# A two-layer encoder trunk: the output projections with one 512-column product per step

## The chip, the core and the metric

The kernel runs on one core of one Trainium2 chip. The metric is device time in microseconds: the median of several executions. TensorE (PE in the profile, its weight loads PEld), VectorE (DVE), ScalarE (ACT), GpSimd (POOL) and SyncE (SP, which here issues the DMAs) each run their own queue of instructions in order and wait for one another by semaphores. TensorE multiplies a 128x128 weight tile, loaded first, with a moving operand of up to 512 columns and adds the result up in PSUM.

## The reference

Two layers over 256 tokens of width 2048. Each layer normalises its input, projects it into the inputs of two groups of heads, computes the groups, gates them, and sends the 2048 gated columns through one output projection whose result is added to the layer's input. A last norm follows.

```python
for l in range(DEPTH):
    h = rms_norm(x, norm_g[l])
    proj = jnp.einsum('btd,dc->btc', h, w_in[l])
    ...                       # RWKV-7 time mixing -> y_rw, windowed attention -> y_at
    mix = jnp.concatenate([y_rw * jax.nn.silu(g_rw), y_at * jax.nn.silu(g_at)], axis=-1)
    x = x + jnp.einsum('btc,cd->btd', mix, w_out[l])
return rms_norm(x, final_g)
```

The change is in the last product, `mix` times `w_out`.

## The kernel before

Everything is kept transposed: 128 channels on the partitions, the 256 tokens along the row. A matrix of width 2048 is thus 16 rows (`kk` or `k` = 0 to 15) of 128x256.

**Products in three parts.** To keep single precision, each operand is split into a high part (rounded to the float32r type that TensorE multiplies in one pass) and a low part (what the rounding left). A product of weight W and operand X is computed as Wh Xh + Wh Xl + Wl Xh: the three lines L309, L310 and L311 of `step` in `gemm`. One output tile of 128 channels is 16 such steps, 48 products, all added up in one PSUM tile `pm` (128x256, two buffers in turn). A weight tile comes in two halves of 8 steps. `wload` (L231) starts the DMA of a half from DRAM into one of three `raw` buffers, `wsplit` makes `hi` on ScalarE (L239) and `lo` on VectorE (L241), in two pieces of 512 columns each, into one of two buffers.

**The stream.** `Stream` holds the list of all weight halves of the whole kernel, input and output projections, and runs one step at a time. PE's order is the order in which the code is written. The scans of the time mixing and the attention are written as generators, and `window` runs pieces of them between steps of the stream. The other engines' instructions are ordered by priorities.

**The output projection.** The gated columns `mix` are 16 rows, split like all operands: the high parts in `MH`, the low parts in `ML`. Rows 0 to 7 (time mixing) are written at the end of `scan_b`, rows 8 to 15 (attention) by `mix_split` (L681 to L683). In the profile the first eight rows are MHa and MLa, the others MHb and MLb. `queue_output` puts 16 tiles (`k`) in the stream. By the counts of the stream, the attention ends just as the first output tile begins; while the output tiles run nothing else is on PE. After a tile's last product, `evac` adds the residual on VectorE (L641) to get the new row x. In layer 0 ScalarE and VectorE split x for the next layer (`x_split`, L203 and L204) and a DMA copies it to DRAM (L650); in both layers ScalarE squares it (L655) and VectorE adds up the squares for the norm (L657). `begin` loads the residual row of a tile from DRAM when the tile begins (L635).

The names in the rows of the profile: pm the PSUM tile, hi and lo the split weights, raw the loaded ones, vg (layer 0) or X2a and X2b (layer 1) the residual row and then the new x, XH and XL the split x of the input projections, mf the squares. L1125, L1112, L216 and L994, which the prediction uses for comparison, are products of the attention (values), its transposes, the sums of the norm and a product of the scan.

Of the kernel before, what the change touches and what calls it, by code (L numbers as in the profile page):

```python
# [21 lines left out]
T = 256  # L22
# [111 lines left out]
def hybrid_trunk_kernel(ctx, tc, xT, wi, wv, wo, par, fing, dup, iup, sink, pos, cst, out):  # L134
# [47 lines left out]
    class Rows:  # L182
# [11 lines left out]
        def __getitem__(self, at):  # L194
# [3 lines left out]
                return self.t[k.start // n][p, k.start % n : (k.stop - 1) % n + 1, t]  # L198
            return self.t[k // n][p, k % n, t]

    def x_split(XH, XL, x, k, l):
        g = G0[:, k : k + 1] if l == 0 else PR[:, l, P_NG + k : P_NG + k + 1]
        A.activation(XH[:, k, :], x, AF.Copy, scale=g)  # L203
        V.scalar_tensor_tensor(XL[:, k, :], x, g, XH[:, k, :].bitcast(F32), op0=ALU.mult, op1=ALU.subtract)  # L204
# [87 lines left out]

    S = Stream()

    def gemm(src, operands, evac, raws=None, begin=None, bank=None):

        box = []

        def step(kk):
            def f(w):  # L300
                if not box:
                    box.append(bank() if bank else ps_main.tile([128, T], F32, tag="m", name="pm"))
                    if begin:
                        begin()
                pm = box[0]
                rh, rl = operands()
                k = kk % 8
                wh, wl = w[0][:, k * 128 : (k + 1) * 128], w[1][:, k * 128 : (k + 1) * 128]
                PE.matmul(pm, wh, rh[:, kk, :], start=(kk == 0), stop=False)  # L309
                PE.matmul(pm, wh, rl[:, kk, :], start=False, stop=False)  # L310
                PE.matmul(pm, wl, rh[:, kk, :], start=False, stop=(kk == 15))  # L311
# [313 lines left out]
    def queue_output(l):  # L625

        L = layers[l]
        last = l + 1 == DEPTH

        def tile_of(k):  # L630
            xs = []

            def begin():
                xs.append(st("vg", [T], bufs=8))
                SY.dma_start(out=xs[0], in_=L.xin[:, k, :])  # L635

            def evac(pm):
                if last and k == 0:
                    L.X2 = Rows("s3", F32, "X2")
                x = L.X2[:, k, :] if last else xs[0]  # L640
                V.tensor_tensor(x, pm, xs[0], op=ALU.add)  # L641
                to = end if last else layers[l + 1]
                if k == 0:
                    to.norm = Norm()
                    to.acc = st("acc", [T])
                    if not last:
                        to.XH, to.XL = Rows("s2", F32R, "XH"), Rows("s3", F32R, "XL")
                if not last:
                    x_split(to.XH, to.XL, x, k, l + 1)
                    SY.dma_start(out=L.xd[:, k, :], in_=x)  # L650
                if k == 0:
                    A.activation(to.acc, x, AF.Square)
                else:
                    sq = st("mf", [T])
                    A.activation(sq, x, AF.Square)  # L655
                    if k < NKT - 1:
                        V.tensor_tensor(to.acc, to.acc, sq, op=ALU.add)  # L657
                    else:
                        to.sums = [to.acc, sq]
                if last:  # L660
                    A.activation(x, x, AF.Identity, scale=FG[:, k : k + 1])
                elif k == NKT - 1:
                    S.later(7, lambda: to.norm.add(to.sums))
                    S.later(14, lambda: to.norm.spread())

            return evac, begin

        for k in range(NKT):
            ev, be = tile_of(k)
            gemm(wo[l, k], lambda: (L.MH, L.ML), ev, begin=be)  # L670

    def layer(l):
        L = layers[l]
        prm = lambda o, j: PR[:, l, o + j : o + j + 1]
        dpm = lambda o, j: DP[:, l, o + j : o + j + 1]
        L.MH, L.ML = MH, ML = Rows("s1", F32R, "MH", 1), Rows("s0", F32R, "ML", 1)
# [294 lines left out]
        def scan_b(p, t):  # L971
# [77 lines left out]
            PA.activation(MH[:, p, :], Zt, AF.Copy)  # L1049
            yield  # L1050
            PV.tensor_tensor(ML[:, p, :], Zt, MH[:, p, :].bitcast(F32), op=ALU.subtract)
            yield

        chains = {}
# [73 lines left out]
        def attend():  # L1128

            scores(0)  # L1130
            yield
            flip(0)
            scores(1)
            yield
            for x in (MH, ML):
                x.more()
# [145 lines left out]
```

## Time and profile before

| | |
|---|---|
| time, median of 3 runs | 1171.67 us (1170.61 to 1172.37) |
| the profiled execution | 1171.01 us, its span 1169.2 us |
| PE busy in the span | 1148.4 us, 16151 products and as many weight loads |
| output projection of layer 0 | about 497 to 588 us of the span |
| output projection of layer 1 | about 1067 to 1157 us of the span |
| DVE, ACT busy | 905.4 us, 785.5 us |

A row of the timeline gives the start in us from the span's start, the duration, the engine, the line of the code, the operation, output<-inputs, the shape and, in brackets, how long the engine sat idle before and for whom. The ends of products are modelled and products overlap: their pace is read from their starts. A row of a tile gives the shortest, median and longest duration in ns and the first and last start in us. The granted clock is the share of TensorE's full clock that the throttle let through.

### The profile page before, as it was taken

What the parts mean: (1) busy time and instruction counts of PE and PEld (TensorE: products, weight loads), DVE (VectorE), ACT (ScalarE), POOL (GpSimd) and SP (SyncE); (2) the same over time, 40 slices, a digit from 0 to 9 for tenths busy, and PEclk for the clock granted to TensorE, in tenths of its full rate; (3) what the DMA queues carried; (4) which work ended last, traced back from release to release, by engine and by line L of the source; (5) the groups of instructions that cost most, each with busy time, mean ns of one, the idle gap of its engine ahead of it and who ended that gap; (6) DMA issues with size and microseconds to landing.
All of it is one profiled execution on the core that took longest, in us unless ns stands there. A gap on an engine that the chain in (4) does not pass through costs nothing.

```text
span 1169.2 us, 38101 instructions
## 1 busy us (share of the span) xinstructions
PE 1148.4 (98%) x16151; PEld 1074.6 (92%) x16151; DVE 905.4 (77%) x2012; ACT 785.5 (67%) x1986; POOL 21.7 (2%) x23
## 2 busy tenths in 40 slices
PE   8999999999999999999999999999999999999996
PEld 7988999999899999899999899999999999899996
DVE  7889978888877677766668888888887767786554
ACT  6667876787776666655556677876786666675553
POOL 0000000000000000000000000000000000000000
PEclk9999999999999999999999999999999999999998
DMA  7544334333333433477655443334333343346653
GB/s 261 168 152 134 130 106 127 97 112 113 96 116 124 134 120 121 141 238 234 212 177 176 141 135 116 106 108 131 98 112 111 121 136 122 106 144 191 213 192 127
DMA packets 60554, 166.63 MB, mean 143 GB/s; under 512 B 7744, under 2 KB 22880, under 8 KB 60384
## 3 DMA queue, kind: packets, MB, share of 16 engines
q1 hardware_dynamic: 60384, 164.21, 43.8%
q8 instruction: 126, 2.06, 0.7%
q14 instruction: 44, 0.36, 0.1%
HBM read 157.37 MB, written 4.19 MB: 138 GB/s over the span
## 4 chain that ended last, share of the span: by engine, by line
PE 75%; issue 13%; DVE 5%; ACT 4%; DMA 1%; SPq 0%; POOL 0%; POOLq 0%; DVEq 0%; ACTq 0%
PE pm L309 19%; PE pm L311 16%; PE pm L310 16%; PE pg L831 3%; PE pcc L994 2%; DVE lo L241 2%; PE pcc L1022 2%; PE pd L938 1%; PE py L1006 1%; PE py L979 1%; PE pq L929 1%; PE pcc L1012 1%; ACT hi L239 1%; DMA raw<-wi 1%; PE pza L689 1%
## 5 line engine op out<-in xcount | busy, mean ns | idle before, releaser
L241 DVE TENSOR_TENSOR lo<-raw,hi 128x512 fp32r<-128x512 f32 x560 | 372.0, 687 | 115.2 <-ACT hi L239 109.8
L239 ACT ACTIVATE hi<-raw 128x512 fp32r<-128x512 f32 x560 | 329.5, 625 | 169.7 <-PE pm L310 98.0
L309 PE MATMUL pm<-XHa,hi 128*128 128x256 f32 x832 | 245.6, 295 | 0.8 <-ACT VA L587 0.4
L309 PE MATMUL pm<-XHb,hi 128*128 128x256 f32 x832 | 243.5, 293 | 0.2
L311 PE MATMUL pm<-XHb,lo 128*128 128x256 f32 x832 | 234.2, 281 | 1.4 <-DVE lo L241 1.4
L311 PE MATMUL pm<-XHa,lo 128*128 128x256 f32 x832 | 234.1, 281 | 1.2 <-DVE lo L241 1.0
L310 PE MATMUL pm<-XLb,hi 128*128 128x256 f32 x832 | 234.0, 281 | 0.4 <-DVE XLb L204 0.4
L310 PE MATMUL pm<-XLa,hi 128*128 128x256 f32 x832 | 234.2, 281 | 0.1
L309 PEld LDWEIGHTS pm<-XHa,hi 128*128 128x128 f32 x832 | 157.1, 189 | 11.4 <-ACT XHa L203 1.3
L309 PEld LDWEIGHTS pm<-XHb,hi 128*128 128x128 f32 x832 | 157.0, 189 | 6.0 <-ACT hi L239 0.3
L311 PEld LDWEIGHTS pm<-XHa,lo 128*128 128x128 f32 x832 | 157.2, 189 | 2.5 <-DVE lo L241 2.4
L311 PEld LDWEIGHTS pm<-XHb,lo 128*128 128x128 f32 x832 | 157.2, 189 | 2.1 <-DVE lo L241 2.0
L310 PEld LDWEIGHTS pm<-XLa,hi 128*128 128x128 f32 x832 | 157.4, 189 | 0.7 <-DVE XLa L204 0.7
L310 PEld LDWEIGHTS pm<-XLb,hi 128*128 128x128 f32 x832 | 157.3, 189 | 0.6 <-DVE XLb L204 0.6
L1017 ACT ACTIVATE suv<-pcc 64x128 f32<-64x128 f32 x128 | 34.5, 270 | 72.3 <-PE pcc L1015 48.4
L309 PE MATMUL pm<-MHa,hi 128*128 128x256 f32 x256 | 72.0, 281 | 0.0
L311 PE MATMUL pm<-MHb,lo 128*128 128x256 f32 x256 | 71.8, 280 | 0.0
L310 PE MATMUL pm<-MLa,hi 128*128 128x256 f32 x256 | 71.8, 280 | 0.0
L310 PE MATMUL pm<-MLb,hi 128*128 128x256 f32 x256 | 71.7, 280 | 0.0
L309 PE MATMUL pm<-MHb,hi 128*128 128x256 f32 x256 | 71.7, 280 | 0.0
L311 PE MATMUL pm<-MHa,lo 128*128 128x256 f32 x256 | 71.7, 280 | 0.0
L309 PEld LDWEIGHTS pm<-MHa,hi 128*128 128x128 f32 x256 | 48.2, 188 | 0.8 <-issue 0.8
(291 smaller groups left out, 2322.7 us busy)
## 6 DMA issues: line engine op xcount, KB each, us to landing
raw<-wi SPq DMA_DIRECT2D x207, 512.0 KB
raw<-wo SPq DMA_DIRECT2D x64, 512.0 KB
raw<-wv SPq DMA_DIRECT2D x8, 512.0 KB
rrot<-u SPq DMA_DIRECT2D x80, 32.0 KB
vg<-xT SPq DMA_DIRECT2D x16, 128.0 KB
xd<-vg SPq DMA_DIRECT2D x16, 128.0 KB
vg<-xd SPq DMA_DIRECT2D x16, 128.0 KB
g<-dup SPq DMA_DIRECT2D x16, 97.0 KB
```

Of the source, the lines that this page charges most:

```text
L239: A.activation(hi[:, q], raw[:, q], AF.Copy)
L241: V.tensor_tensor(lo[:, q], raw[:, q], hi[:, q].bitcast(F32), op=ALU.subtract)
L309: PE.matmul(pm, wh, rh[:, kk, :], start=(kk == 0), stop=False)
L310: PE.matmul(pm, wh, rl[:, kk, :], start=False, stop=False)
L311: PE.matmul(pm, wl, rh[:, kk, :], start=False, stop=(kk == 15))
L689: PE.matmul(o, w[0], x[0], start=True, stop=False)
L831: PE.matmul(pg[:, h, c * 128 : (c + 1) * 128], BK[half[h], d, c, 1 - h : 3 - h, :].rearrange("p s j -> p (s j)"), MV[half[h], d, c].rearra ...
L929: PE.matmul(narrow(pq[:, d], h ^ d, c), hq(AB, d, c, h), sub(TC, h, d, c, d * b), start=True, stop=True)
L938: PE.matmul(narrow(pd[:, d], h, c), hx(TT, d, c, h), sub(QF, h ^ d, d, c, d * b), start=True, stop=True)
L994: PE.matmul(pc[half[h], 0, d, :], GE[h][r, d, ci[d], 0, :], SUV[r, d, ci[d], h, :], start=True, stop=True)
L1017: A.activation(here(h), pc[half[h], 1], AF.Copy)
L1022: PE.matmul(pS[half[h], d, :], BT[:, h, d, i, :], SUV[:, d, ci[d], h, :], start=(i == 0), stop=True, skip_group_check=True)
```

## The change

The split rows of `mix` no longer lie in two arrays, high and low, but side by side: row `kk` of `L.M` (class `Pairs`, four rows per tile, tiles M0 to M3) is 512 columns, 256 high and then 256 low. In 15 of 16 output tiles of each layer (`wide`) `pm` is 128x512, and a step has two products: the high weights with all 512 columns (Wh Xh into the first half, Wh Xl into the second), and the low weights with the 256 high columns, added to the first half. The evacuation then takes two additions on VectorE: residual plus first half, and that plus second half. The last tile of each layer keeps three products and one addition.

```diff
+    class Pairs:
+        def more(self):
+            for tag in (("s0a", "s1a"), ("s0b", "s1b"))[len(self.t) // 2]:
+                self.t.append(hold(tag, F32R, "M" + str(len(self.t)), (4, 2, T)))
+        def row(self, j, part=None):
+            t = self.t[j // 4][:, j % 4]
+            return t.rearrange("p a t -> p (a t)") if part is None else t[:, part]
...
-                    box.append(bank() if bank else ps_main.tile([128, T], F32, tag="m", name="pm"))
+                    box.append(bank() if bank else ps_main.tile([128, 2 * T if wide else T], F32, tag="m", name="pm"))
...
+                if wide:
+                    m = pairs()
+                    PE.matmul(pm, wh, m.row(kk), start=(kk == 0), stop=(kk == 15), skip_group_check=True)
+                    PE.matmul(pm[:, 0:T], wl, m.row(kk, 0), start=False, stop=(kk == 15), skip_group_check=True)
+                    return
...
-                V.tensor_tensor(x, pm, xs[0], op=ALU.add)
+                V.tensor_tensor(x, pm[:, 0:T], xs[0], op=ALU.add)
+                if k < NKT - 1:
+                    V.tensor_tensor(x, x, pm[:, T : 2 * T], op=ALU.add)
...
-            gemm(wo[l, k], lambda: (L.MH, L.ML), ev, begin=be)
+            gemm(wo[l, k], None, ev, begin=be, pairs=lambda: L.M, wide=k < NKT - 1)
...
-            A.activation(MH[:, j, :], mf, AF.Copy)
-            V.tensor_tensor(ML[:, j, :], mf, MH[:, j, :].bitcast(F32), op=ALU.subtract)
+            A.activation(L.M.row(j, 0), mf, AF.Copy)
+            V.tensor_tensor(L.M.row(j, 1), mf, L.M.row(j, 0).bitcast(F32), op=ALU.subtract)
```

On PE, the end of layer 0's first output tile (step 15) and the first step of the second stand so before:

```order
L309 MATMUL pm_9537<-MHb_8529,hi_9560 128x256 [waits Activation_49]
L310 MATMUL pm_9537<-MLb_8530,hi_9560 128x256 [waits DVE_49]
L311 MATMUL pm_9537<-MHb_8529,lo_9561 128x256
L309 MATMUL pm_9614<-MHa_331,hi_9592 128x256 [waits Activation_49]
L310 MATMUL pm_9614<-MLa_332,hi_9592 128x256
L311 MATMUL pm_9614<-MHa_331,lo_9593 128x256 [waits DVE_49]
```

and so in the changed kernel:

```order
L324 MATMUL pm_9537<-M3_8530,hi_9554 128x512 [waits DVE_49]
L325 MATMUL pm_9537<-M3_8530,lo_9555 128x256
L324 MATMUL pm_9599<-M0_331,hi_9578 128x512 [waits Activation_49]
L325 MATMUL pm_9599<-M0_331,lo_9579 128x256 [waits DVE_49]
L324 MATMUL pm_9599<-M0_331,hi_9578 128x512
```

Three products of a step have become two; the waits for the split weights stand at the same places. On VectorE, between two output tiles of layer 0, before:

```order
L657 TENSOR_TENSOR acc_9605<-acc_9605,mf_9685 128x256
L241 TENSOR_TENSOR lo_9744<-raw_9741,hi_9743 128x512 x2
L641 TENSOR_TENSOR vg_9689<-pm_9688,vg_9689 128x256
L241 TENSOR_TENSOR lo_9786<-raw_9783,hi_9785 128x512 x2
L204 SCALAR_TENSOR_TENSOR XLa_9608<-vg_9689,PR_83,XHa_9606 128x256
```

and in the changed kernel:

```order
L681 TENSOR_TENSOR acc_9590<-acc_9590,mf_9655 128x256
L255 TENSOR_TENSOR lo_9700<-raw_9697,hi_9699 128x512 x2
L663 TENSOR_TENSOR vg_9659<-pm_9658,vg_9659 128x256
L665 TENSOR_TENSOR vg_9659<-vg_9659,pm_9658 128x256
L255 TENSOR_TENSOR lo_9735<-raw_9732,hi_9734 128x512 x2
L218 SCALAR_TENSOR_TENSOR XLa_9593<-vg_9659,PR_83,XHa_9591 128x256
```

The second addition stands right behind the first, ahead of the next low parts. No instruction of ScalarE or GpSimd has moved; on SP one load of a residual row stands ahead of a copy to DRAM that it followed before.

More of the change, by code (lines that the diff above doesn't have):

```diff
@@ L199, in __getitem__, with __init__ @@
             return self.t[k // n][p, k % n, t]
+    class Pairs:
+        def __init__(self):
+            self.t = []
+            self.more()
+        def more(self):
[4 more added lines that the diff above has]
+            return t.rearrange("p a t -> p (a t)") if part is None else t[:, part]
     def x_split(XH, XL, x, k, l):
@@ L293, in hybrid_trunk_kernel, with gemm @@
     S = Stream()
-    def gemm(src, operands, evac, raws=None, begin=None, bank=None):
+    def gemm(src, operands, evac, raws=None, begin=None, bank=None, pairs=None, wide=False):
         box = []
@@ L305, in f @@
                 pm = box[0]
-                rh, rl = operands()
                 k = kk % 8
                 wh, wl = w[0][:, k * 128 : (k + 1) * 128], w[1][:, k * 128 : (k + 1) * 128]
-                PE.matmul(pm, wh, rh[:, kk, :], start=(kk == 0), stop=False)
-                PE.matmul(pm, wh, rl[:, kk, :], start=False, stop=False)
-                PE.matmul(pm, wl, rh[:, kk, :], start=False, stop=(kk == 15))
+                if wide:
[3 more added lines that the diff above has]
+                    return
+                if pairs:
+                    xh, xl = (pairs().row(kk, i) for i in range(2))
+                else:
+                    xh, xl = (x[:, kk, :] for x in operands())
+                PE.matmul(pm, wh, xh, start=(kk == 0), stop=False)
+                PE.matmul(pm, wh, xl, start=False, stop=False)
+                PE.matmul(pm, wl, xh, start=False, stop=(kk == 15))
             return f
@@ L1048, in scan_b @@
             yield
-            PA.activation(MH[:, p, :], Zt, AF.Copy)
+            PA.activation(L.M.row(p, 0), Zt, AF.Copy)
             yield
-            PV.tensor_tensor(ML[:, p, :], Zt, MH[:, p, :].bitcast(F32), op=ALU.subtract)
+            PV.tensor_tensor(L.M.row(p, 1), Zt, L.M.row(p, 0).bitcast(F32), op=ALU.subtract)
             yield
@@ L1134, in attend @@
             yield
-            for x in (MH, ML):
-                x.more()
+            L.M.more()
             for j in range(8):
```

2 lines of the change are left out of this document (1 added, 1 removed).

## The prediction, made before the run

> **What bounds the kernel now.** I read the page first, for which engine is full and what the chain that ended last is made of.
>
> ```profile
> span 1169.2 us, 38101 instructions
> PE 1148.4 (98%) x16151; PEld 1074.6 (92%) x16151; DVE 905.4 (77%) x2012; ACT 785.5 (67%) x1986; POOL 21.7 (2%) x23
> ...
> GB/s 261 168 152 134 130 106 127 97 112 113 96 116 124 134 120 121 141 238 234 212 177 176 141 135 116 106 108 131 98 112 111 121 136 122 106 144 191 213 192 127
> ...
> PE 75%; issue 13%; DVE 5%; ACT 4%; DMA 1%; SPq 0%; POOL 0%; POOLq 0%; DVEq 0%; ACTq 0%
> ```
>
> TensorE is full, and every product has a weight load of its own (16151 of each). Then the stretches of the two output projections, by windows (length, then busy time and instructions of PE, PEld, DVE, ACT and POOL, granted clock, DMA share, GB/s):
>
> ```profile
> 497.00:588.00 91.00, 91.00 (x769) 91.00 (x768) 59.12 (x111) 47.24 (x95) 0.00 (x0) 1.00 0.71 227
> 1066.50:1157.00 90.50, 90.50 (x774) 90.13 (x769) 52.35 (x94) 48.16 (x94) 0.00 (x0) 1.00 0.59 188
> ```
>
> In both, PE and its loads have no gap at a granted clock of 1.00, VectorE is busy 59 and 52 us of 91, and the DMA engines 0.71 and 0.59. So time goes here only as products go. Their pace comes from the first and last start of the first product of a step (tile MHa, in each window):
>
> ```profile
> L309 PE MATMUL pm<-MHa,hi x128: 277/281/388, 497.0 to 585.0; 128*128 128x256 f32 x128
> L309 PE MATMUL pm<-MHa,hi x128: 277/280/389, 1066.9 to 1153.9; 128*128 128x256 f32 x128
> ```
>
> The last MHa row is step 7 of the 16th tile, 247 steps after the first. So a step of three products takes 88.0/247 = 356.3 ns in layer 0 and 87.0/247 = 352.2 ns in layer 1: 118.8 and 117.4 ns a product, whatever the 281 ns that a row calls its duration (products overlap). The timeline shows it, with the work of the other engines beside it:
>
> ```profile
> 559.80 1.15 ACT L239 ACTIVATE hi<-raw 128x512 fp32r<-128x512 f32 x2 [1.65 <-PE pm L310]
> 559.92 0.42 DVE L641 TENSOR_TENSOR vg<-pm,vg 128x256 f32<-128x256 f32 x1 [0.96 <-PE pm L311]
> 560.20 0.28 PE L310 MATMUL pm<-MLa,hi 128*128 128x256 f32 x1
> 560.20 0.19 PEld L311 LDWEIGHTS pm<-MHa,lo 128*128 128x128 f32 x1
> 560.31 0.28 PE L311 MATMUL pm<-MHa,lo 128*128 128x256 f32 x1
> 560.47 1.29 DVE L241 TENSOR_TENSOR lo<-raw,hi 128x512 fp32r<-128x512 f32 x2
> 561.68 0.48 DVE L204 SCALAR_TENSOR_TENSOR XLb<-vg,PR,XHb 128x256 fp32r<-128x256 f32 x1
> 562.08 0.42 DVE L657 TENSOR_TENSOR acc<-acc,mf 128x256 f32<-128x256 f32 x1
> 562.45 0.19 PEld L309 LDWEIGHTS pm<-MHb,hi 128*128 128x128 f32 x1
> ```
>
> The next weights start loading as a product starts: load and columns run side by side, and the slower of the two, plus whatever they cost each other, sets the 118 ns.
>
> **The change, part by part.** In 15 of 16 tiles of each layer a step loses one product and one weight load: 2 x 15 x 16 = 480 of each. What remains is one product of 512 columns and one of 256. The whole forecast is the price of the 512-column product at full clock, and no row of before has one with these operands. Four rows bound it. The first is a stretch in which the clock was halved:
>
> ```profile
> 297.30:300.70 3.40, 3.40 (x21) 3.18 (x24) 3.13 (x9) 2.93 (x8) 0.00 (x0) 0.51 0.02 6
> 298.16 0.41 PE L309 MATMUL pm<-XHb,hi 128*128 128x256 f32 x1
> 299.87 0.41 PE L311 MATMUL pm<-XHb,lo 128*128 128x256 f32 x1
> ```
>
> Eight products of the same form in 1.71 us are 213.8 ns each at half clock, so the columns alone would take 106.9 ns at full clock; 118 is some 11 ns more than the columns need. What are these 11 ns? Three readings, each with its price for 512 columns.
>
> - The weight load sets the pace. Then a wide product hides the next load whole and costs its columns: 2 x 106.9 = 214, and 216 by a row of the nearest kind, products of twice the array time per column (attention values) that start 0.22 us apart with a load begun under them:
>
> ```profile
> 1031.81 0.38 PE L1125 MATMUL po<-pp,VA 128*64 128x256 f32 x1
> 1032.03 0.38 PE L1125 MATMUL po<-pp,VA 128*64 128x256 f32 x1
> 1031.81 0.14 PEld L1125 LDWEIGHTS po<-pp,VA 128*64 128x64 f32 x1
> ```
>
> Against it: loads of products with one column each (the norm's sums) follow at (0.53 - 0.19)/3 = 0.113 us, below 118; and a product followed by a transpose, whose load is recorded with 141 ns where these have 188, still holds the next one back for 0.12 us.
>
> ```profile
> 590.22 0.53 PEld L216 LDWEIGHTS pr<-C,acc 128*128 128x128 f32 x4
> L1112 PEld LDWEIGHTS ppt<-C,mv x112: 137/141/145, 418.0 to 1063.4; 128*128 128x128 f32 x112
> 458.20 0.28 PE L311 MATMUL pm<-XHb,lo 128*128 128x256 f32 x1
> 458.32 0.60 PE L1112 MATMUL ppt<-C,mv 128*128 128x128 f32 x4
> ```
>
> - The 11 ns are a charge per product (taking over new weights, or one load getting in the columns' way). A wide product pays it once: 106.9 + 118.8 = 225.7 ns.
> - The 11 ns are a charge per column: at full clock these operands can't be fed faster than 118/256 = 0.46 ns a column. Then 512 columns cost 2 x 118 = 236 and nothing is won. Against it: where PE must empty before it takes another layout, the next load starts 0.20 us after the last of these products, and 0.31 us after a product of twice the array time per column:
>
> ```profile
> 881.57 0.28 PE L311 MATMUL pm<-XHb,lo 128*128 128x256 f32 x1
> 881.77 0.26 PEld L994 LDWEIGHTS pcc<-suv,ge 128*64 128x64 f32 x6
> ...
> 1032.29 0.38 PE L1125 MATMUL po<-ip,VA 128*64 128x256 f32 x1
> 1032.60 0.19 PEld L1085 LDWEIGHTS pscr<-KA,kr 64*128 64x128 f32 x2 [0.39 <-issue]
> ```
>
> 0.22 - (0.31 - 0.20) = 0.11 us are left for the columns of a product that has no load beside it: less than 118, though the rounding of four starts makes it a lean and no proof.
>
> I take the middle, 225.7: it is the one that neither the short load nor the drained product contradicts. A step then saves 118.8 - 106.9 = 11.9 ns in layer 0 and 117.4 - 106.9 = 10.5 ns in layer 1: 240 x 11.9 + 240 x 10.5 = 5.4 us.
>
> The Trainium skill, TensorE: Matmul & The Clock Gate, "Back-to-back issue gap", gives N/2.4 + 2.5 ns for an isolated product: 109 at 256 columns and 216 at 512. Its 109 is not what this trace shows (118). Taken for all products it would make this change worth 2.5 ns a step, an estimate of 1.2 us; taken for the wide one alone it is the first reading.
>
> The rest lies beside this. VectorE gets 30 more additions, no nearer row than L657 and L641 (0.42 us each from SBUF and from PSUM): 12.6 us in all, one per tile. They stand ahead of the next tile's low parts. VectorE now has 2 x 1.29 + 2 x 0.42 + 0.48 = 3.9 us a tile of 5.7 and would have 4.3 of 5.5. The low part of the first 512 weights ends at 560.47 + 0.65 = 561.1 and PE comes to it at 562.45 + 0.24: a lead of 1.5 us. The addition takes 0.45 of it, the shorter half tile 0.1; 0.95 us is left, so I cost it at nothing, and above a delay of 0.95 us each further one would be paid in full. ScalarE's high part at 562.7 waited for PE, not PE for it. The copy to DRAM of layer 0 waits for the second addition on SP's queue, 0.45 us later, with weight loads behind it; layer 0's stage would ask 227 x 356/344 = 235 GB/s, and the page's first slice moves 261, so the loads keep up, and I leave 0.5 us in the range for one that comes late. One residual load moves ahead of a copy; its row is read a tile later. Splitting the mixed rows writes as many elements as before to other places. The first wide product wants both parts of its row where before the first wanted the high one; the last row is written long before step 15.
>
> Sum: the profiled execution took 1171.01 us (span 1169.2, 1.8 around it), 0.66 below the median 1171.67. 1171.67 - 5.4 = 1166.3.
>
> **The rivals.**
> - Load-bound (first reading): a step becomes 216 + 118.8 = 334.8 and 216 + 117.4 = 333.4; saved 240 x 21.5 + 240 x 18.8 = 9.7 us: 1162.0. For it, the load starting with the product and the 216 row; against it, the short load. 0.2.
> - Charge per column (third reading), the change not doing what it seems to: 1171.7. For it, that 118 held before a short load too; against it, the drained product. 0.25.
> - A wide product costing hardly more than a narrow one, 118: 480 x 118 = 57 us saved, 1115. At half clock products take their columns exactly, which speaks against it. 0.01. The same section of that skill page gives 131 ns sustained at N = 512, which is this rival.
> - Slower: the low parts come late. Place: VectorE at a tile's start, where the two additions wait for the tile's last product and hold the low parts back. It decides from a delay of 0.95 us past today's. If the second addition waited as the first does today (0.96 us idle before L641), the lead would be gone by 0.5 us in 30 tiles: +15 - 5.4, 1181. Against it, that nothing the second addition needs comes later than what the first waited for. 0.06.
>
> **How the numbers follow.** Middle reading 0.48, load-bound 0.2, per column 0.25, hardly more 0.01, slower 0.06. 0.2% is 2.3 us, about what a measurement of this kernel can tell from no change. Faster: 0.48 + 0.2 + 0.01, and 0.03 of the per-column case if small savings add up: 0.72; same 0.22; slower 0.06. The likeliest case alone runs from 1164.5 to 1168. The range must take in the load-bound time and the no-change time: 1161.5 to 1171.7.
>
> **What would show it.** PE with 15671 products, 480 fewer. In the output stages, the step of a wide tile: 344 and 341 ns if I am right, 334 if load-bound, 353 if per column; with it the wide product's start to the narrow one's, 225 or 216 or 236. The narrow product to the next wide one stays at 118. Low parts: no wait of PE for DVE lo at a tile's first steps; if there is one, the slower rival is at work. Outside these stages nothing moves. I am wrong if the stages shrink by less than 1 us each, or if PE shows gaps in them.

## The result: 2.4 us faster, where 5.4 were forecast

The changed kernel takes 1169.07 us (median of 15 runs, 1166.21 to 1170.37) against 1171.44 us before (15 runs, 1170.18 to 1174.78) on the same chip: a ratio of 0.9976 with a 95% interval of 0.9968 to 0.9984, so 1.9 to 3.7 us saved. On another chip (experiment e11) it was 1168.44 against 1171.50, 0.9968 (0.9955 to 0.9981). The time lies inside the forecast range, the sign is right, and the gain is a little under half of what was forecast.

The page of the profile after, its first lines and the chain that ended last:

```profile
span 1166.7 us, 37155 instructions
PE 1145.5 (98%) x15671; PEld 1051.1 (90%) x15671; DVE 915.9 (79%) x2042; ACT 785.6 (67%) x1986; POOL 21.7 (2%) x23
...
PE 76%; issue 13%; DVE 5%; ACT 4%; DMA 2%; SPq 0%; POOL 0%; POOLq 0%; DVEq 0%; ACTq 0%
```

480 products and 480 weight loads are gone, 30 additions have come, and the span is 2.5 us shorter. TensorE is as full as before. The two output stages by windows (length, then busy time and instructions of PE, PEld, DVE, ACT and POOL, granted clock, DMA share, GB/s), and the rows of the wide product (line 324) in them:

```profile
496.70:586.70 90.00, 89.41 (x530) 78.92 (x529) 64.26 (x126) 47.39 (x95) 0.00 (x0) 1.00 0.72 229
1065.70:1154.50 88.80, 88.80 (x528) 78.85 (x529) 56.91 (x109) 47.69 (x93) 0.00 (x0) 1.00 0.62 191
...
L324 PE MATMUL pm<-M,hi x240: 391/392/500, 496.7 to 580.8; 128*128 128x512 f32 x120
L324 PE MATMUL pm<-M,hi x240: 391/392/502, 1065.6 to 1148.6; 128*128 128x512 f32 x120
```

In layer 1 PE has no gap, and 239 steps take 83.0 us: 347.3 ns a step, where 341 (341.7 by its sum) was forecast (without one start that came 0.11 us late the records give 346.7). In layer 0 the same 239 steps take 84.1 us, and the window shows 0.59 us in which PE did nothing. It waited twice there (the list has what waited, what for, and then us in all, times, longest):

```profile
PE pm L324 <- ACT hi L253: 0.4, 1, 0.4
PE pm L325 <- DVE lo L255: 0.2, 1, 0.2
```

The list counts from the modelled ends of products, so it shows less than was lost: by the starts, these two products came 0.52 us (the one that waited for hi) and 0.50 us (the one that waited for lo) later than usual, and the next one 0.10 us.

From the start of a stage's first product to the first product behind the stage, by the records of the two traces (the starts of single products in ns; the views round them):

| stage | before | after | saved |
|---|---|---|---|
| layer 0 | 91.24 us | 90.07 us | 1.17 us |
| layer 1 | 90.22 us | 88.94 us | 1.28 us |
| layer 0's stage to layer 1's | 478.67 us | 478.84 us | -0.17 us |

So the gain is in the two stages, as it should be (the first also begins 0.27 us sooner, 496.69 for 496.96, no more than traces of one kernel differ: e11, the same code again, begins it at 496.61, and e4 and e10, alike up to there, at 497.68 and 497.47). Two things are to be explained: a step that is dearer than forecast, and about 1 us lost in layer 0.

The spacing of starts within a step, from the records (single spacings more than 15 ns off the median, at most two of a kind in a stage, left out):

| | before, layer 0 | before, layer 1 | after, both layers |
|---|---|---|---|
| wide product to the narrow one | | | 229.2 ns |
| narrow product to the next | 118.7 ns | 117.3 ns | 117.5 ns |
| step | 356.0 ns | 352.0 ns | 346.7 ns |
| saved in a step | 9.3 ns | 5.3 ns | |

240 x 9.3 + 240 x 5.3 = 3.5 us, less about 1.0 us of stalls in layer 0, is the 2.5 us by which the span fell.

### The profile page after: what moved, and what is told of

Read it like the earlier page. It is cut to its first block, busy times and chain, and to the rows that moved or that the text cites. A ratio compares the mean times of both kernels' runs of the same rounds, so it can differ in the third digit from the quotient of the medians.

```text
span 1166.7 us, 37155 instructions
## 1 busy us (share of the span) xinstructions
PE 1145.5 (98%) x15671; PEld 1051.1 (90%) x15671; DVE 915.9 (79%) x2042; ACT 785.6 (67%) x1986; POOL 21.7 (2%) x23
## 4 chain that ended last, share of the span: by engine, by line
PE 76%; issue 13%; DVE 5%; ACT 4%; DMA 2%; SPq 0%; POOL 0%; POOLq 0%; DVEq 0%; ACTq 0%
PE pm L331 17%; PE pm L333 14%; PE pm L332 14%; PE pm L324 4%; PE pg L855 3%; PE pm L325 2%; PE pcc L1018 2%; DVE lo L255 2%; PE pcc L1046 2%; PE pd L962 1%; PE py L1030 1%; PE py L1003 1%; PE pq L953 1%; PE pcc L1036 1%; ACT hi L253 1%
## 5 line engine op out<-in xcount | busy, mean ns | idle before, releaser
L324 PE MATMUL pm<-M,hi 128*128 128x512 f32 x480 | 166.9, 392 | 0.4 <-ACT hi L253 0.4
L325 PE MATMUL pm<-M,lo 128*128 128x256 f32 x480 | 134.3, 280 | 0.2 <-DVE lo L255 0.2
L324 PEld LDWEIGHTS pm<-M,hi 128*128 128x128 f32 x480 | 90.1, 188 | 21.2 <-issue 0.8
L325 PEld LDWEIGHTS pm<-M,lo 128*128 128x128 f32 x480 | 90.1, 188 | 0.5 <-DVE lo L255 0.5
L1124 ACT ACTIVATE mv<-mv,mx 128x257 f32<-128x257 f32 x56 | 28.0, 502 | 15.1 <-DVE mx L1121 15.0
L956 ACT ACTIVATE QF<-pq 128x256 f16<-128x256 f32 x80 | 30.4, 380 | 10.5 <-PE pq L920 6.2
L855 PE MATMUL pg<-mv,FR 64*128 64x128 f32 x512 | 37.2, 285 | 0.0
```

Of the source, the lines that this page charges most:

```text
L324: PE.matmul(pm, wh, m.row(kk), start=(kk == 0), stop=(kk == 15), skip_group_check=True)
L325: PE.matmul(pm[:, 0:T], wl, m.row(kk, 0), start=False, stop=(kk == 15), skip_group_check=True)
L855: PE.matmul(pg[:, h, c * 128 : (c + 1) * 128], BK[half[h], d, c, 1 - h : 3 - h, :].rearrange("p s j -> p (s j)"), MV[half[h], d, c].rearra ...
L956: A.activation(t_sub(QF), flat4(pq[:, :, 0:128]), AF.Copy)
L1124: A.activation(Sc[:, h, q, 0:257], Sc[:, h, q, 0:257], AF.Exp, scale=0.125, bias=mx[:, q : q + 1], accum_out=den[:, q : q + 1])
```

## Experiments on the price of a step

Three kernels carry, behind the end of the changed kernel, series of 24 to 96 products on an otherwise quiet core. They take fp32r rows from the tiles M of layer 1, as the kernel does; nothing reads what they compute. The first, e1:

```
+ W = lambda c: lambda i: M.row(i)[:, 0:c]          # weights, c columns
+ X = lambda n: lambda i: M.row(i)[:, 0:n]          # moving rows, n columns
+ for n in (512, 384, 256, 128, 64): series(24, W(128), X(n))
+ series(24, W(128), X(512), X(256))
+ for n in (512, 256): series(24, W(64), X(n))
+ for n in (512, 256, 128): f16 operands from QF, 128 weight columns
+ 512 and 256 again with VectorE, with ScalarE and with 8 loads of 512 KB beside
```

> The changed kernel with series of products of one size behind its end (24 or 48 each, results not used), so its time is longer by the series, about 150 us, and only the spacing within a series counts. Theory M (from the changed kernel's trace: 117.5 ns for 256 columns, 229.3 for 512): beside the columns' own time at the full clock (106.7 ns for 256) a product pays about 5 ns once and about 5.5 ns per 256 columns. It gives 229 at 512, 173 at 384, 117.5 at 256, 62 at 128 (or more, if the weight load then sets the pace). Theory P (the prediction's, all 11 ns paid once per product): 224 at 512 in a quiet series, 171 at 384, 118 at 256, 65 at 128; the 4 to 5 ns more at 512 in the kernel then came from other engines. Theory C (all paid per column): 235, 176, 118, 59. Theory X (contention with the other engines' traffic makes the extra): quiet series at 213 and 107, and 230 and 118 only while DVE, ACT or the loads work beside. If the extra is paid for loading weights, 64 columns of weights (half a load) lower the once-paid part; if it belongs to the four-byte rows, f16 products show 213 and 107.

Rows of single series, by line and window; a row's first and last start, divided by its count less one, is the spacing (0.1 us of rounding is 4 ns there, so the numbers in the text are from the records):

```profile
L1232 PE MATMUL probe<-M,M x23: 334/334/346, 1176.7 to 1180.5; 128*128 128x384 f32 x23
L1232 PE MATMUL probe<-M,M x23: 278/283/283, 1180.8 to 1183.5; 128*128 128x256 f32 x23
L1232 PE MATMUL probe<-M,M x22: 273/274/277, 1183.8 to 1186.1; 128*128 128x128 f32 x22
L1232 PE MATMUL probe<-QF x24: 379/379/390, 1201.4 to 1206.3; 128*128 128x512 f16 x24
L1232 PE MATMUL probe<-QF x22: 272/273/273, 1206.8 to 1209.1; 128*128 128x256 f16 x22
...
L1232 PE MATMUL probe<-M,M x27: 389/389/389, 1220.8 to 1226.7; 128*128 128x512 f32 x27
L1232 PE MATMUL probe<-M,M x27: 389/389/389, 1242.9 to 1248.8; 128*128 128x512 f32 x27
L1232 PE MATMUL probe<-M,M x27: 389/389/389, 1265.0 to 1270.9; 128*128 128x512 f32 x27
```

Quiet, fp32r: 227 ns at 512 columns, 174 at 384, 119.4 at 256, 111.7 at 128 and at 64 (without the first spacing of these two). Weights of 64 columns give 229.6 ns at 512 and 113.4 at 256. The last three rows are 512 columns with VectorE, with ScalarE and with loads beside: 5.9 us for 26 spacings in each, 227 ns. So theory X falls: the other engines have no part in it. With f16 rows the same series give 216.3, 109.2 and 55.8 ns: there a product costs its columns (106.9 ns per 256, by the half-clock row of the prediction) and some 2.4 ns, so most of the extra belongs to fp32r operands. A plain series of one size fits theory P's form (13 ns over the columns at 512, 12.5 at 256), theory M less well; theory C's 235 is off. It also fits the prediction's own rule: 120 + 106.9 is 226.9. But 512 and 256 in turn took 231 to 233 and 112 to 118 here, over and over 117, 231, 112, 233 ns, which is 346.7 ns a pair, just what the kernel's own pair takes: a product's price depends on what stands beside it, and no single number of a plain series gives the price of its wide product. The second kernel, e5, ran the steps themselves, more sizes, and short weights:

```
+ series(24, (W(0), X(0)), (W(0), X(1)), (W(1), X(0)))   # the old step
+ series(24, (W(0), R()), (W(1), X(0)))                   # the new pair
+ for n in (448, 320, 288, 224, 192): series(24, (W(), R(n)))
+ for n in (512, 384, 256, 128): series(24, (W(n=32), R(n)))
```

> The changed kernel with further series of products behind its end, results not used; only the spacings count. Quiet series so far: 227 ns at 512 columns, 173 at 384, 119.4 at 256, so about 13.4 ns per product beside the columns' own time, and a floor of 111 at 128 and 64. Theory P2 (one charge per product, 13.4 ns whatever it is beside): the kernel's old step of three 256-column products takes 3 x 120 = 360 ns here, the new pair 347; 448, 320 and 288 columns give 200, 147 and 133. Theory S (the charge hangs on what stands beside the product, so that it is 11 in the old step and 13.4 in the new): 353 to 356 for the three, 347 for the pair, and the series with fixed operands or with the same weights twice differ from 227 and 119.4 by some ns. Theory F (256 columns last hardly longer than the load's floor, which then sets their pace): 224 and 192 columns stay at 111 or more instead of 107 and 93, and weights of 32 columns, a quarter of the load, bring 128 columns down to some 60 ns and 256 to 110, while 512 stays at 227 or more.

```profile
L1231 PE MATMUL probe<-M,M x21: 272/274/280, 1215.7 to 1217.9; 128*128 128x224 f32 x21
L1231 PE MATMUL probe<-M,M x21: 272/273/278, 1218.3 to 1220.6; 128*128 128x192 f32 x21
...
L1231 PE MATMUL probe<-M,M x23: 388/392/398, 1221.0 to 1226.1; 128*32 128x512 f32 x23
L1231 PE MATMUL probe<-M,M x22: 280/281/282, 1230.7 to 1233.2; 128*32 128x256 f32 x22
L1231 PE MATMUL probe<-M,M x20: 222/223/226, 1233.6 to 1234.7; 128*32 128x128 f32 x20
```

The old step takes 360.0 ns, just three times 120 (P2 holds); the pair 353.3 (P2's 347 is missed, S's too), though the pair of e1 had it. There each product had weights and a row of its own; here the two of a pair share their row, as in the kernel. Two pairs in the order wide, wide, narrow, narrow take 697.2 ns, 348.6 a pair. Fixed operands gave 227 and 120 ns, and the same weights in both products of the pair 353.3, so a change of weights or rows is not what makes the plain series or this pair take what they do. With weights of 128 columns 224 and 192 columns both take 111.8 ns (theory F's floor); with weights of 32 columns the floor is gone, 128 columns take 60.0. The Trainium skill, TensorE: Matmul & The Clock Gate, "LDWEIGHTS (loading the stationary operand)", has a load last by its columns, P/1.2: by that rule an estimate of 107 ns for 128 columns. The floor of 111.8 ns for fp32r and its going agree with that; the f16 series of e1, at 55.8 ns with weights of 128 columns, do not show such a floor. But F's second half misses: at 256 columns short weights still take 117.8, not 110, and the four sizes 60.0, 117.8, 173.0 and 231.1 lie nearly on a line, 57 ns per 128 columns and 3 ns once. With these weights the extra is paid mostly by the column (57.0 for 53.4 ns), which is the third reading of the prediction. It is no rule for short loads: with weights of 64 columns (e1) the extra is 6.5 ns at 256 and 15.8 at 512, with 32 columns 10.9 and 17.3.

The third, e12, asked why the kernel's own steps (353.7 as the mean of the input projections, 346.7 for the pair) lie 6.5 ns below those of e5:

```
+ hl = (WH, WL): weights in tiles of their own, as hi and lo
+ for w in (M, hl): for acc in (summed up, started anew):
+     series(32, *three(w), acc=acc);  series(32, *pair(w), acc=acc)
+ the same two steps with f16 operands
```

> The changed kernel with series behind its end again, results not used: the old step of three 256-column products and the new pair, each (a) summed up in one PSUM tile as in the kernel or started anew with every product, and (b) with the weights in a tile of their own, as the kernel's hi and lo, or in the tile beside the moving rows, as in the series so far (three: 360 ns, pair: 353). In the kernel the three take 353.7 and the pair 346.7, so both steps lie 6.5 ns lower there. Theory A (it is the summing up): 354 and 347 wherever the products are summed up, whatever the weights' place. Theory B (it is the weights' place): 354 and 347 with the weights in a tile of their own. Neither: 360 and 353 in all four, and then the saving of a step, 7 ns, is the same in all although the steps themselves differ. With f16 operands, where no extra per column was seen (109 at 256, 216 at 512), three products should take 327 and the pair 325, a saving of 2 ns only.

The old step and the pair, weights in M and summed up; then the f16 ones; and the clock of the first series:

```profile
L1232 PE MATMUL probe<-M,M x93: 283/283/284, 1169.1 to 1180.1; 128*128 128x256 f32 x93
L1232 PE MATMUL probe<-M,M x62: 277/340/404, 1180.6 to 1191.3; 128*128 128x256 f32 x31, 128*128 128x512 f32 x31
L1232 PE MATMUL probe<-QF x70: 272/273/273, 1260.4 to 1267.9; 128*128 128x256 f16 x70
L1232 PE MATMUL probe<-QF x48: 272/326/380, 1268.0 to 1275.7; 128*128 128x512 f16 x24, 128*128 128x256 f16 x24
...
1169.00:1180.00 11.00, 11.00 (x94) 11.00 (x93) 0.00 (x0) 0.00 (x0) 0.00 (x0) 1.00 0.01 1
```

All four ways of fp32r gave 360.0 and 353.3 ns: "neither". What makes the steps shorter in the kernel stays open. That nothing else runs beside the quiet pair is not it, since the pair of e1 was as quiet and took 346.7.

The traces do show that one and the same step has more than one pace. In the input projections of before, after, e4 and e6, every unbroken run of ten old steps or more goes at 352 or at 356 ns (one at 357), and the same run can go at the one in one kernel and at the other in another. The first products of four tiles at the start of layer 1, 55 steps from first to last, in before and then in e4:

```profile
L309 PE MATMUL pm<-XHa,hi x32: 277/280/282, 595.2 to 614.6; 128*128 128x256 f32 x32
...
L331 PE MATMUL pm<-XHa,hi x32: 277/281/283, 593.6 to 613.2; 128*128 128x256 f32 x32
```

19.4 and 19.6 us; by the records the unbroken run of 63 steps there goes at 352.0 and at 356.0 ns a step. So the 356 and 352 ns of the two output stages are two paces of one step. The pair, too, has been seen at two, 346.7 and 353.3 ns, though not with the same operands. What the change saves in a step is the difference of the paces that the old and the new step happen to run at:

| step | three products | pair | saved |
|---|---|---|---|
| quiet series, fp32r (e5, and four ways in e12) | 360.0 ns | 353.3 ns | 6.7 ns |
| quiet series, fp32r (e1) | | 346.7 ns | |
| input projections of e9, by the records | 354.0 ns | 347.1 ns | 6.9 ns |
| output stages, layers 0 and 1 | 356.0 and 352.0 ns | 346.7 ns | 9.3 and 5.3 ns |
| quiet series, f16 | 327.5 ns | 325.0 ns | 2.5 ns |

The 768 columns of a step are 3 x 106.9 = 320.7 ns. In the quiet series of e5 and e12 three products pay 39.3 ns beside them and two pay 32.6, so a product less saves 6.7 ns. A fixed share for the product and a fixed share for its columns does not follow: by such a split a plain series of 512 columns would take 233 ns, and it takes 227. The Trainium skill, TensorE: Matmul & The Clock Gate, "Back-to-back issue gap", which the prediction cites, gives by N/2.4 + 2.5 an estimate of 109 and 216 ns, and 131 ns sustained at 512 columns. The f16 series here agree with the formula (109.2, 216.3), the fp32r ones do not (119.4, 227), and no series came near the 131.

## Experiments on the rest of the change

**The layout alone** (e2): tiles M as in the change, three narrow products everywhere.

```
- gemm(wo[l, k], None, ev, begin=be, pairs=lambda: L.M, wide=k < NKT - 1)
+ gemm(wo[l, k], None, ev, begin=be, pairs=lambda: L.M, wide=False)
- if k < NKT - 1: V.tensor_tensor(x, x, pm[:, T : 2 * T], op=ALU.add)
```

> The new layout of the operand rows with the old step of three 256-column products everywhere, no second addition. Theory M: the gain is the wide product's alone, so the time is that of the kernel before (1171.4 us, ratio 1.000 within 0.001), 15 tiles of three products at 353 to 356 ns a step. Rival (the layout itself gives or takes time, since high and low rows now lie in the same tile): a ratio off 1 by over 0.001, 1169 us if the layout were the whole gain.

1171.91 us against 1171.87, ratio 1.000 (0.999 to 1.001), stages of 91.44 and 90.22 us. The layout gives and takes nothing; theory M holds. (0.20 of layer 0's 91.44 us are two products that came 0.10 us late at the start of its fifth tile, behind the late load of which e4 tells.)

**Without the second addition** (e3):

```
- if k < NKT - 1: V.tensor_tensor(x, x, pm[:, T : 2 * T], op=ALU.add)
```

> The changed kernel without the second addition, so the product with the low rows is left out of the result in 15 tiles of 16. Theory M: the 30 additions lie beside the products, and the time stays at the changed kernel's 1169.1 us within 0.6 (ratio 0.998). Rival D (the additions push the low parts of the weights back and cost the missing 3 us of the prediction): about 1166 us, ratio 0.9955, and no idle time of PE behind DVE in layer 0's output stage.

1167.87 us, ratio 0.9964 (0.9952 to 0.9977). That is below theory M's 1169.1 and above rival D's 1166, and its interval meets that of the changed kernel (0.9968 to 0.9984): by the time it is undecided. The trace is plainer. Layer 1's stage is 88.94 us, as with the addition; layer 0's is 89.63, 0.44 us shorter, and PE's waits in it (the whole list) are down to one:

```profile
PE pm L325 <- DVE lo L255: 0.2, 1, 0.2
```

So the additions cost nothing in 29 of 30 tiles. Nor do the records give them a share in the stalls of layer 0's fifth tile. The stall on lo is 0.50 us in every trace with the additions and the load unheld (after, e1, e5, e11, e12) and 0.50 us here without them, though at step 8 of the tile instead of step 0, since here the load came late that brings the tile's other half of weights. What differs is the stall on hi: 0.52 us (after), 0.40 (e11), 0.34 (e1), 0.95 (e5) none in e12 and 0.08 here. It comes and goes with the load's lateness: e12, which keeps the additions, has a stage of 89.55 us, less than the 89.63 here.

**The late load** (e4). In layer 0's stage of the changed kernel SP's queue, and what followed 4.7 us behind it:

```profile
509.37 0.43 SPq L533 DMA_DIRECT2D g<-iup  x1
509.85 0.31 SPq L533 DMA_DIRECT2D g<-dup  x1
510.25 3.89 SPq L245 DMA_DIRECT2D raw<-wo  x1
...
518.83 1.15 ACT L253 ACTIVATE hi<-raw 128x512 fp32r<-128x512 f32 x2 [3.44 <-DMA raw<-wo]
518.87 0.28 PE L325 MATMUL pm<-M,lo 128*128 128x256 f32 x1
519.49 0.69 DVE L255 TENSOR_TENSOR lo<-raw,hi 128x512 fp32r<-128x512 f32 x1 [3.03 <-ACT hi L253]
519.51 0.49 PE L324 MATMUL pm<-M,hi 128*128 128x512 f32 x1 [0.36 <-ACT hi L253]
```

A weight load that is issued in 0.33 to 0.38 us elsewhere in the stage took 3.89 us, right behind layer 1's first iup and dup rows, which stand behind the stage in the program and are issued in its third tile. ScalarE waited 3.44 us for it, and PE for ScalarE. The stall on lo follows from that: VectorE can start on the low part only behind the high one and takes 0.69 us, and the wide product, the only one of its step that needs no low part of the weights, covers 0.23 us of it. The kernel before shows the same throughout: of its 16 pairs of iup and dup loads, 12 have a load right behind them that took 1.0 to 3.2 us to issue. In this stage it took 3.18 us, and PE got by:

```profile
510.52 3.18 SPq L231 DMA_DIRECT2D raw<-wo  x1
...
518.28 1.16 ACT L239 ACTIVATE hi<-raw 128x512 fp32r<-128x512 f32 x2 [2.19 <-DMA raw<-wo]
```

In the trace of e3 the two loads stand apart, and it is dup (97 rows of the tile) and not iup (96) that has the slow issue behind it, there at least; why, no run shows:

```profile
508.61 0.43 SPq L533 DMA_DIRECT2D g<-iup  x1
509.40 0.34 SPq L245 DMA_DIRECT2D raw<-wo  x1
...
512.70 0.28 SPq L533 DMA_DIRECT2D g<-dup  x1
513.08 2.77 SPq L245 DMA_DIRECT2D raw<-wo  x1
```

The edit holds both loads to their place in the program, behind the stage:

```
+ d = SY.dma_start(out=t[n][0:rows], in_=src[l, ...])
+ if l and not p: tc.keep_in_program_order(d)
```

> The changed kernel with layer 1's first pair of iup and dup loads held to their place in the program, behind layer 0's output stage; before, they were issued in its third tile, just ahead of the wo load that took 3.9 us to issue. Theory L: these small-packet loads make that wo load late, and the two stalls of 0.50 and 0.52 us go: output stage of layer 0 89.0 us instead of 90.1, time 1168.1 us (ratio 0.9972). Rival Q (the load is late because the queue is full of wo and xT loads anyway, or the stall moves to the start of layer 1's input projections): stage of 90 us or a new wait of PE behind iup, and 1169.1 us or more.

Layer 0's stage took 88.95 us (89.0 expected), the same as layer 1's 88.94; the list of PE's waits in it is empty, and the loads in that place are issued in 0.33 us:

```profile
511.20 0.33 SPq L245 DMA_DIRECT2D raw<-wo  x1
...
L324 PE MATMUL pm<-M,hi x240: 391/392/500, 497.7 to 580.6; 128*128 128x512 f32 x120
```

82.9 us for 239 steps, against 84.1. The time was 1167.88 us, ratio 0.9958 (0.9944 to 0.9971). Theory L holds in the trace; the time agrees with it, but its interval meets the changed kernel's. The two loads now stand behind the stage, where the weight load behind them takes 2.98 us to issue in its turn, but nothing is lost by it: from layer 0's stage to layer 1's it is 478.75 us, against 478.84.

**The same in the kernel before** (e6): the edit of e4 on the old step.

> The kernel before with layer 1's first pair of iup and dup loads held to their place in the program. Theory L: PE did not stall behind that load in the kernel before, its columns being slower, so nothing is gained: 1171.5 us, ratio within 0.001 of 1, output stage of layer 0 at 91.2 us. Rival (the held loads save 1 us wherever they are, so that the gain of the changed kernel with them is not owed to the change): ratio 0.999 or less, 1170.4 us.

1171.48 us against 1171.69, ratio 0.9999 (0.9988 to 1.001); stages of 91.24 and 90.22 us, just as before. So the microsecond was not there to be had: the load was late before too, and it became a stall of 1 us only when PE came to its tile sooner (0.20 us at the most with the old step, in e2).

**Held loads and no second addition** (e10), beside **the changed kernel again** (e11):

> The changed kernel with the held loads and without the second addition, so the product with the low rows is left out of the result in 15 tiles of 16. Theory L: with the wo load in time the additions cost nothing, so the output stages stay at 88.95 and 88.94 us and the time at that of the run with held loads alone, 1167.9 us within 0.6. Rival D (the additions cost time of their own beside the late load): 1166.5 us or less.

> The changed kernel as it is, beside the two others on one chip. Theory L: 1169.1 us within 0.7, about 1 us above the run with held loads alone (1167.9), its output stages at 90.1 and 88.9 us again. Rival (the difference of the two was one of chips or of rounds): the same time as the run without the second addition and with held loads, and no stall in layer 0's output stage.

e10: stages of 88.95 and 88.94 us, as e4; with the load in time the additions cost nothing. e11: stages of 89.95 and 88.94 us, with PE's two waits back in layer 0 (the whole list):

```profile
PE pm L324 <- ACT hi L253: 0.2, 1, 0.2
PE pm L325 <- DVE lo L255: 0.2, 1, 0.2
```

By the time the two can't be told apart: 1168.35 us (0.9966, 0.9953 to 0.9979) and 1168.44 (0.9968, 0.9955 to 0.9981). The microsecond is shown by the stage and not by the time of whole runs: layer 0's took 89.55 to 90.50 us in the six traces of kernels with the load unheld (after, e1, e3, e5, e11, e12) and 88.94 or 88.95 in the five with it held (e4, e7 to e10). Layer 1's took 88.94 us in all of them but one: 90.01 in e1, where PE waited 0.8 us for the low part of a mixed row, which VectorE made late because a fill that belongs to the added series had come ahead of it.

## Experiments on doing more of it

If a pair saves 6.7 ns wherever it stands, the 1664 steps of input projections should be worth more than the outputs. The rows XH and XL were laid side by side too, the loads of e4 held, and first the 32 gate tiles (e7), then k, v and r as well (e8) got the pair. ScalarE copies the half with the low rows out of PSUM, and VectorE adds the other:

```
- V.tensor_tensor(g, pm, L.norm.rb, op=ALU.mult)
+ A.activation(g, pm[:, T : 2 * T], AF.Copy)
+ V.tensor_tensor(g, g, pm[:, 0:T], op=ALU.add)
+ V.tensor_tensor(g, g, L.norm.rb, op=ALU.mult)
- inproj(5 + 4 * p, silu_evac(...))
+ inproj(5 + 4 * p, silu_evac(...), wide=True)        # and so in the other tiles
```

> The changed kernel with the held loads, and the 32 gate tiles of the input projections with the pair of products as well: the rows XH and XL lie side by side too, and each such tile has one more copy by ScalarE and one more addition by VectorE. By the pair's measured step (347 against 353.7 ns) 512 steps save 3.2 us: 1164.7 us, ratio 0.9935 against the kernel before. Rival V (VectorE and ScalarE, busy beside, get late with the tiles or the weights' parts): no gain over the run with held loads alone (1167.9, ratio 0.996), PE waiting for lo or for a pm buffer by some us more.

> As the run with wide gate tiles, and the 48 tiles of k, v and r too: 80 tiles or 1280 steps with the pair, 80 more copies by ScalarE and 80 more additions by VectorE, most of them in the stage where the scans keep both engines busy. If all lies beside the products: 1280 x 6.3 = 8.1 us less than with held loads alone, 1159.8 us, ratio 0.990. Rival V: the added work (80 x some 0.7 us on VectorE) delays the scans' chains, PE waits for them, and the time is above that of the run with gate tiles alone.

1173.62 us (ratio 1.0014, 1.0002 to 1.0026) and 1195.14 us (1.0196, 1.0175 to 1.0217): both slower than before, and for e7 worse than rival V had it. The largest waits of PE, of e7 and then of e8:

```profile
PE pm L348 <- DVE lo L270: 4.7, 4, 1.9
PE pbn L747 <- DVE ip L283: 4.5, 2, 2.3
...
PE py L1090 <- DVE ysq L283: 12.2, 8, 2.2
PE pm L339 <- ACT hi L268: 7.2, 2, 3.8
PE pm L340 <- DVE lo L270: 5.2, 9, 1.2
```

The steps themselves got their 6 to 7 ns (347.8 against 354.0 in e7). But all gaps of PE over 0.15 us add up to 19.6 us in e7 and 38.2 in e8, against 11.7 in e4, most of them behind VectorE: the low parts of weights and the scans' chains wait behind the added evictions. The clock takes a part, too: from 7 us of the span to the last norm the trace of e4 has 6.8 us at a granted clock of 0.5, e7 has 10.2 and e8 23.9, so that, as an estimate at half a microsecond lost for each, 1.7 and 8.5 us more are lost than in e4. For e8 that is 26.4 us of gaps and 8.5 of clock, less 1280 x 6.7 ns = 8.6, or some 26 us, and its span is 26.3 us longer than e4's. The output stages of both stayed at 88.94 us. The last one (e9) took only the 8 gate tiles of each layer that lie in the attention stage.

> The changed kernel with the held loads, and of the input projections only the 8 gate tiles of each layer that lie in the attention stage (g0 to g7) with the pair of products: 256 steps, 16 more copies by ScalarE and 16 more additions by VectorE. VectorE is 73 to 77% busy there, against 84 to 88% in the scans' stage where the wide tiles cost more than they gave. If the added work is hidden: 256 x 6.7 ns = 1.7 us less than with held loads alone, 1166.2 us, ratio 0.9943 against the kernel before. Rival V: the two waits of 0.5 us each that the run with all gates wide had at 461 to 466 us stay, and the rest of the gain goes too: 1167.3 to 1168 us.

1168.10 us, ratio 0.9968 (0.9957 to 0.9979): no gain that can be told from e11 on the same chip (0.9968). By the trace, 0.86 us was to be had in each layer (128 steps); layer 0's output stage began 0.17 us earlier than in e4 (497.51 for 497.68), and layer 1's 0.28 us sooner after it (478.47 us for 478.75), which is little more than the 0.21 and 0.19 us by which e4 and e10, the same code there, differ. In layer 0 a wait at the attention values stayed (ahead of its output stage, the whole list):

```profile
PE po L1171 <- ACT pp L1162: 0.4, 1, 0.4
PE pm L348 <- DVE lo L270: 0.2, 1, 0.2
```

These take 0.6 of the 0.86 us; where the rest of layer 1's went was not found. The lowest ratio of a kernel with the whole result is that of e4, the change with the two loads held (0.9958), but its interval meets those of the change alone and of e9.

## Why the forecast was half right

- **TensorE sets the end, and time goes only as products go.** Right: 480 products less, nothing moved outside the stages beyond what traces of one kernel differ by, layout worth nothing (e2).
- **The 512-column product at 225.7 ns.** This is the term that was mis-sized: "the 11 ns are a charge per product". The wide product takes 229.2, and a step saves 9.3 and 5.3 ns, not 11.9 and 10.5: 3.5 us instead of 5.4. The prediction took one price from narrow products among their like and carried it over to a wide one between narrow ones. Among its like the wide product does follow the rule (227 ns quiet, 226.9 by the rule); between narrow ones it takes 229 in the kernel and 232 or 236 in the quiet series. f16 operands show none of this. What sets the spacing of fp32r products in a mixed series, no run shows.
- **The rivals on that price.** Load-bound, 216 ns: no; a floor set by the load exists (111.8 ns) but lies under the 256-column product. Per column, 236 ns: not in the kernel, though the quiet pair of e5 and e12 has its wide product at 236 on average. "Hardly more than a narrow product": no. The drained product of the prediction (0.11 us) was a sound hint that the columns alone are fast, but said nothing on how the rest is shared.
- **What made layer 0's old step 4 ns longer than layer 1's** (356.0 and 352.0, also in e2 and e6, while the pair takes 346.7 in both) was taken as it was. It is no property of layer 0: the input projections have both paces, and the last tile of layer 0's stage in the changed kernel, which keeps the old step, takes 351.9. That the saving was 9.3 ns there and not 5.3 is thus luck as far as the runs show. Why a stretch runs at one pace and not at the other stays open.
- **30 additions at nothing.** Right: in 29 tiles of the changed kernel PE waited for nothing, in the one with the late load the stall on lo is as long without them (e3), and with that load in time they cost nothing (e10).
- **"The loads keep up, and I leave 0.5 us for one that comes late."** One came late, and it cost 1.0 us: two stalls, on hi and on lo. The GB/s of the stage was the wrong row for this; the row to see was on SP's queue, an issue of 3.18 us where others of the stage take 0.33, with layer 1's iup and dup loads ahead of it. It stood in the trace of before. By the prediction's own sign ("or if PE shows gaps in them") it was wrong here.
- **The low parts late as a slower rival.** Its sign came, a wait for lo at a tile's first step, but not its cause: it is one wait and not 30, and it stands behind the late load.

Put together: 5.4 forecast, less 1.9 for the price, less 1.0 for the load, is 2.5 us by the trace. That the time lies inside the range says little for the price: the range reached from the load-bound time to no change.

## What to carry to other kernels

A spacing above the columns' own time is not a charge that goes away with the product: price the step as a whole, old and new, before counting on the difference. A quiet series behind the kernel's end gives its order (6.7 ns here), but one step can have two paces a few ns apart, so what it saves in place is read in place (9.3 and 5.3 ns). When the bounding engine gets faster, look in the queue of loads for the one that is already late with no one waiting, since it is the next stall. And an addition that is free beside one stage can cost more than it brings beside another: the pair gained in the output stages, and in 80 tiles of the input projections, with a copy and an addition in each, it made the kernel 23 us slower than before.

## What the hardware showed that was not expected

At a granted clock of 1.00, fp32r products with weights of 128 columns are spaced 227 ns at 512 columns, 202 to 203 at 448, 173 to 174 at 384, 147 at 320, 132 at 288, 120 at 256 and 112 from 224 down to 64. f16 products take 216, 109 and 56 ns at 512, 256 and 128. A wide fp32r product that stands between narrow ones takes longer than among its like: in the quiet pair of e5 and e12 the spacings run through 240, 120, 236, 114, 233, 117 ns, a pattern of three pairs, though the rows repeat after eight, and 236 on average against 227; in that of e1 they run through 231, 112, 233, 117, a pattern of two. Steps of three narrow products go at 352 or 356 ns in the kernel and at 360 in the quiet series. What sets these patterns, and which of them a stretch falls into, no run here shows.
